# A trunk of Mamba-2, attention and FFN layers: weight loads on ScalarE's queue, scratch tensors in the reader's layout, decay work recorded later

## The chip, the cores and the metric

The kernel runs on one core of a Trainium2 chip. The metric is the device time of one execution in microseconds (us): 3116.06 us before, the median of three runs (3113.17 to 3118.34). The execution that was profiled took 3113.31 us; its span, from the first to the last instruction, is 3111.6 us. Everything is computed in float32. To keep the accuracy, each large matrix product is made of three matmuls on reduced-precision parts: a tensor `t` is split into a high part and the remainder, and the product is high x high + high x low + low x high.

Engines: PE is TensorE (matmul), ACT is ScalarE, DVE is VectorE, POOL is GpSimd, SP is SyncE. SP does no arithmetic; in the kernel before it issues almost all DMAs. Each engine takes its instructions in the order in which they stand on it, and one that waits holds up all behind it.

## The reference, cut to what matters

One sequence of 1024 tokens with 1024 channels passes four residual layers: Mamba-2 mixer, FFN, attention, FFN. The change lies mostly in the mixer:

```
def ssd_mixer(xn, in_w, ...):
    proj = xn @ in_w                       # z, xbc, dt
    xbc = silu(causal_dwconv(xbc, conv_w, conv_b))     # 4 taps along time
    dt = softplus(dt + dt_bias); a = -exp(a_log)
    a_cs = cumsum(dt * a) inside a chunk
    lmat = exp(a_cs[l] - a_cs[s]) for l >= s, else 0   # decay inside the chunk
    y_diag = (C B^T * lmat) @ (x * dt)
    states = B, decay to the chunk's end, x * dt ; h = scan over the chunks
    y_off = C @ h_in * exp(a_cs)
    y = (y_diag + y_off + x * d_skip) * silu(z)
    return (rmsnorm of y inside each of 4 groups * norm_g) @ out_w

x = x + ssd_mixer(rmsnorm(x), ...);   x = x + conv_ffn(rmsnorm(x), ...)
x = x + diff_attention(rmsnorm(x), ...);  x = x + conv_ffn(rmsnorm(x), ...)
```

There are 32 heads of 64 channels in 4 groups of 8 heads; the state has 128 columns; B and C are shared inside a group.

## The kernel before

**Tiles and passes.** Channels lie on the 128 partitions, time on the free axis, in two halves of 512 tokens. A weight block is 128 output channels by 1024 inputs: `split_weight` loads it (`ws`), ACT casts the high part (`wh`, L96), POOL subtracts to get the low part (`wl`, L98). `ws`, `wh` and `wl` have two buffers each. A pass is one 128x128 piece of the weight against 512 tokens: three matmuls (L276 to L278). A projection unit is eight passes into one PSUM tile, after which its end function (`xbc_end`, `z_end`, `out_end`) copies the result out and works on it.

**The mixer's stream.** `Stream` writes the projection passes out one after another, with hooks between them. First come the 40 blocks of the input projection, group by group: six of xbc and four of z. After an xbc block ACT and DVE run the convolution and SiLU (L415 to L427) and SP writes the block to the DRAM scratch `xbc_d` (L428); z blocks go to `z_d` (L439). Then come the 32 blocks of the output projection.

**The core in slots.** The recurrence is worked out in chunks of 128 tokens: 4 groups x 8 chunks are 32 slots, s = 0 to 31, spread between the passes of the stream: 20 passes to a slot for the first 24, 14 for the last eight. For a slot, `core_load` brings `xc` (six blocks of xbc, L539) and `seg` (the cumulated decays of 8 heads, broadcast to all partitions, L541), and records the decay chain: POOL subtracts (L542), ACT applies relu and exp (L543, L544). `core_load_out` brings `er` (L553) and `zc` (L555). `core_tokens` transposes B and x on PE (`pb`, `px`, L568 to L572), copies `btok` on ACT (L574), makes `cbm` and `xdt` on DVE (L576, L579), `xdec` on POOL (L581) and multiplies `seg` by `cbm` on DVE (L582). `core_out` has the products: `pd` (y_diag, L600, reads that `seg`), `po` (y_off, L604), `pst` (the new state, L608), then the sums on DVE and POOL (`y`, L616 to L620; `hn`, L613, L614). The gate multiplies by `zc`, writes `y_d` (L630) and sums squares into `ss` (L632 to L634); after each fourth chunk `group_stats` takes the column sums on PE (`tst`, L149). `out_load` reads `y_d` back as `yb` (L660), scales it and splits it into `xh` and `xl` (L663 to L665) for the output projection.

**What sets the order.** The code records the instructions in a program order; the tile framework's scheduler then sets each engine's own order from it and from the dependencies, so that an instruction can stand earlier on its engine than in the code. A load recorded two slots ahead waits on SP for its buffer (`xc` and `seg` have three) and for whatever stands before it on SP. The four PSUM buffers of the core (`cps`) go round among `pb`, `px`, `pd`, `po`, `pst`, `tst` and others in the order in which they are asked for.

**Attention** runs its projections and output projection through the same `Stream`, between the tiles of scores.

## Time and profile before

| | |
|---|---|
| median of three runs | 3116.06 us |
| the profiled execution, own time / span | 3113.31 us / 3111.6 us |
| mixer, up to the end of the output projection | about the first 940 us |
| busy over the span: PE, DVE, ACT, POOL | 94%, 59%, 34%, 35% |
| the chain that ended last, by engine | PE 67%, DVE 13%, DMA 7%, POOL 4%, issue 3%, ACT 3% |

The profile's page cuts the span in 40 slices. PE is busy in 100% of nearly every slice of the two FFN layers, in some 94% in attention, and least in the mixer. Busy time is only half of what to read there: TensorE's granted clock is the other. Its two levels are 2.4 and 1.2 GHz, shown as 1.00 and 0.50, and the mean over a stretch says how much of it ran at the lower one. A wait is told by the engine that idled, the instruction that ended the idling, and the one that released it. For DMAs the page gives the median time from issue to landing.

### The profile page before, as it was taken

Reading aid. Unit: us, or ns where it says so; the run is one execution under the profiler, and the core shown is the slowest. Engines: PE = TensorE matmul, PEld = TensorE weight load, DVE = VectorE, ACT = ScalarE, POOL = GpSimd, SP = SyncE. Lnnn points to the kernel's source line nnn. Section 1 sums busy time; section 2 is a strip of 40 time slices with the busy share of each in tenths; the row PEclk is TensorE's granted clock in tenths of the full one; section 3 lists DMA queues with packets and bytes.
Section 4 is the critical chain, followed back from the end, with each engine's and each line's share of the span. In section 5 each row is a group of like instructions: output and inputs, shape, how many; then the busy total and the mean of one; then the engine's idle time right before and its main releaser. Section 6 shows DMA issues by size and latency. Waiting matters only on the chain.

```text
span 3111.6 us, 35613 instructions
## 1 busy us (share of the span) xinstructions
PE 2927.5 (94%) x13636; PEld 2312.8 (74%) x13636; DVE 1826.6 (59%) x2880; ACT 1064.2 (34%) x1767; POOL 1076.3 (35%) x776
## 2 busy tenths in 40 slices
PE   7998888887899999999998999999999999999999
PEld 5777677665678888888886666666677888888887
DVE  6436464554666544435357788888867635344354
ACT  4433343433333221212123555555544312122121
POOL 3235454545544222222223633343435222222222
PEclk9999999998899999999999999999999999999999
DMA  3445455556432111111113221122442111111113
GB/s 102 132 122 150 131 144 155 126 158 160 139 107 68 48 48 48 48 48 49 53 39 117 74 57 55 55 61 55 119 144 69 54 48 49 54 48 48 48 45 105
DMA packets 196762, 262.77 MB, mean 84 GB/s; under 512 B 17777, under 2 KB 132977, under 8 KB 196593
## 3 DMA queue, kind: packets, MB, share of 16 engines
q1 hardware_dynamic: 187760, 244.77, 26.1%
q0 software_dynamic: 8832, 15.73, 2.1%
q8 instruction: 107, 1.75, 0.2%
q14 instruction: 63, 0.51, 0.1%
HBM read 206.39 MB, written 45.68 MB: 81 GB/s over the span
## 4 chain that ended last, share of the span: by engine, by line
PE 67%; DVE 13%; DMA 7%; POOL 4%; issue 3%; ACT 3%; SPq 0%; POOLq 0%; ACTq 0%; DVEq 0%
PE mm L112 10%; PE mm L113 10%; PE mm L111 10%; PE dp L112 5%; PE dp L113 5%; PE dp L111 5%; PE mm L276 5%; PE mm L277 5%; PE mm L278 5%; DMA seg<-acs_d 4%; PE s L1120 2%; PE s L1119 1%; POOL seg L542 1%; DVE nb L1122 1%; DVE nb L1123 1%
## 5 line engine op out<-in xcount | busy, mean ns | idle before, releaser
L98 POOL TENSOR_TENSOR wl<-ws,wh 128x1024 fp32r<-128x1024 f32 (+2 forms) x272 | 611.7, 2249 | 1154.8 <-ACT wh L96 1144.9
L276 PE MATMUL mm<-xh,wh 128*128 128x512 f32 x1280 | 539.8, 423 | 16.0 <-ACT xh L664 10.7
L112 PE MATMUL mm<-xl,wh 128*128 128x512 f32 x1408 | 549.1, 390 | 0.6 <-POOL xl L238 0.6
L113 PE MATMUL mm<-xh,wl 128*128 128x512 f32 x1408 | 548.9, 390 | 0.3 <-POOL wl L98 0.3
L111 PE MATMUL mm<-xh,wh 128*128 128x512 f32 x1408 | 548.8, 390 | 0.0
L278 PE MATMUL mm<-xh,wl 128*128 128x512 f32 x1280 | 512.8, 401 | 7.9 <-POOL wl L98 7.9
L277 PE MATMUL mm<-xl,wh 128*128 128x512 f32 x1280 | 513.8, 401 | 3.1 <-DVE xl L238 2.4
L96 ACT CAST wh<-ws 128x1024 fp32r<-128x1024 f32 (+2 forms) x272 | 266.9, 982 | 677.3 <-PE dp L112 296.5
L773 DVE TENSOR_SCALAR cv<-raw,fcw,fcb 128x1024 f32<-128x1024 f32 x88 | 214.9, 2442 | 405.3 <-ACT raw L768 405.3
L276 PEld LDWEIGHTS mm<-xh,wh 128*128 128x128 f32 x1280 | 247.6, 194 | 83.3 <-issue 18.9
L112 PEld LDWEIGHTS mm<-xl,wh 128*128 128x128 f32 x1408 | 265.0, 188 | 57.2 <-POOL xl L238 2.2
L113 PEld LDWEIGHTS mm<-xh,wl 128*128 128x128 f32 x1408 | 264.9, 188 | 55.8 <-POOL wl L98 0.8
L111 PEld LDWEIGHTS mm<-xh,wh 128*128 128x128 f32 x1408 | 265.0, 188 | 54.9
L278 PEld LDWEIGHTS mm<-xh,wl 128*128 128x128 f32 x1280 | 246.7, 193 | 63.0 <-POOL wl L98 10.5
L277 PEld LDWEIGHTS mm<-xl,wh 128*128 128x128 f32 x1280 | 247.3, 193 | 61.7 <-issue 9.1
L809 DVE TENSOR_TENSOR x<-x,dp 128x512 f32<-128x512 f32 x192 | 130.6, 685 | 245.7 <-PE dp L113 245.7
L112 PE MATMUL dp<-al,wh 128*128 128x512 f32 x704 | 274.0, 389 | 0.0
L111 PE MATMUL dp<-ah,wh 128*128 128x512 f32 x704 | 273.9, 389 | 0.0
L113 PE MATMUL dp<-ah,wl 128*128 128x512 f32 x704 | 273.9, 389 | 0.0
L775 DVE SCALAR_TENSOR_TENSOR cv<-raw,fcw,cv 128x1024 f32<-128x1024 f32 x176 | 230.1, 1307 | 12.8 <-DVE cv L773 1.4
L768 ACT COPY raw<-mm 128x512 f32<-128x512 f32 x176 | 101.5, 577 | 189.0 <-PE mm L113 189.0
L421 DVE SCALAR_TENSOR_TENSOR cv<-raw,cw,cv 128x1024 f32<-128x1024 f32 x72 | 111.4, 1548 | 91.3 <-ACT cv L419 61.7
(244 smaller groups left out, 4079.6 us busy)
## 6 DMA issues: line engine op xcount, KB each, us to landing
ws<-in_ffn_up_w_dram SPq DMA_DIRECT2D x88, 512.0 KB, 3.5
ws<-in_ssd_in_w_dram SPq DMA_DIRECT2D x40, 512.0 KB, 3.6
seg<-acs_d SPq DMA_DIRECT2D x32, 512.0 KB, 9.6
ws<-in_ssd_out_w_dram SPq DMA_DIRECT2D x32, 512.0 KB, 3.5
ws<-in_ffn_down_w_dram SPq DMA_DIRECT2D x32, 512.0 KB, 3.4
xbc_d<-cv SPq DMA_DIRECT2D x24, 512.0 KB, 4.1
xc<-xbc_d SPq DMA_DIRECT2D x32, 384.0 KB, 8.0
ws<-in_attn_in_w_dram SPq DMA_DIRECT2D x24, 512.0 KB, 3.5
```

The costliest lines, as they stand in the source:

```text
L96: act.copy(wh[:, :n], ws[:, :n])
L98: pool.tensor_tensor(wl[:, :n], ws[:, :n], wh[:, :n], op=ALU.subtract)
L111: pe.matmul(ps, wh[:, m, k, :], xh, start=k == 0, stop=False)
L112: pe.matmul(ps, wh[:, m, k, :], xl, start=False, stop=False)
L113: pe.matmul(ps, wl[:, m, k, :], xh, start=False, stop=k == n - 1)
L276: pe.matmul(ps, wh[:, 0, k, :], xh, start=k == 0, stop=False)
L277: pe.matmul(ps, wh[:, 0, k, :], xl, start=False, stop=False)
L278: pe.matmul(ps, wl[:, 0, k, :], xh, start=False, stop=k == nk - 1)
L421: dve.scalar_tensor_tensor(cv, raw[:, 1 + k:1 + k + T], cw[:, i, k:k + 1], cv, op0=ALU.mult, op1=ALU.add)
L773: dve.tensor_scalar(cv, raws[b][:, 4:], cw[:, n, 2:3], cb[:, n:n + 1], op0=ALU.mult, op1=ALU.add)
L775: dve.scalar_tensor_tensor(cv, raws[b][:, 2 + k:2 + k + T], cw[:, n, k:k + 1], cv, op0=ALU.mult, op1=ALU.add)
L809: dve.tensor_tensor(x, x, ps, op=ALU.add)
```

## The change

Five things change in the code.

1. `split_weight` is parted: `load_weight` issues the load on a queue that is handed over, and `Stream` keeps `raw`, the loads made so far. Weights of the mixer and of attention are now issued by ACT; `weight(i)` also records the load of block i + 1. The FFN's weights stay on SP.
2. The scratch tensors have the reader's layout. `xbc_d`, `z_d`, `y_d` are stored by group and chunk, so that what a slot reads of one partition lies in one piece; `acs_d` too, with the heads of `er` put side by side. So `xc`, `seg`, `er`, `zc` and the write of `y_d` move one piece for each partition, where they moved 6, 8, 4, 4 and 4 pieces of 512 bytes. The writes of `xbc_d` and `z_d` move eight pieces of 512 bytes for each partition, where they moved one of 4 KB, and the read `yb` four, where it moved one of 2 KB. `acs_d` is written by 16 DMAs in place of two.
3. The decay chain is recorded by `core_decay` at the start of the slot before its use, no longer behind its load.
4. The group's statistics: every chunk has its own `tst` matmul and an ACT copy into `rstd` (`chunk_stats`), one slot later; after the fourth the rsqrt follows on DVE. `out_load(1, h)` moves to the next slot as well.
5. The step at 4/5 of a slot is gone; what it held is in `late`.

```diff
@@ -88,10 +88,16 @@
     gffn = load_const("norm_ffn_g", [P, DEPTH, KB])
-    def split_weight(src, kb, mb):
+    def load_weight(src, kb, mb, queue=None):
         n = kb * mb * P
         ws = wpool.tile([P, 1024], F32, name="ws", tag="ws")
-        sp.dma_start(ws[:, :n], src)
+        (queue or sp).dma_start(ws[:, :n], src)
+        return ws
+
+    def split_weight(src, kb, mb, ws=None):
+        n = kb * mb * P
+        if ws is None:
+            ws = load_weight(src, kb, mb)
         wh = wpool.tile([P, 1024], F32R, name="wh", tag="wh")
         act.copy(wh[:, :n], ws[:, :n])
         wl = wpool.tile([P, 1024], F32R, name="wl", tag="wl")
@@ -246,8 +252,9 @@
-        def __init__(self, wsrc):
+        def __init__(self, wsrc, queue):
             self.wsrc, self.w, self.units, self.hooks = wsrc, {}, [], []
+            self.queue, self.raw = queue, {}
         def add(self, w, nk, xs, end, ahead=0, ps_new=ps_mm):
@@ -257,9 +264,16 @@
             self.hooks.append((n, k, len(self.hooks), f))
             self.hooks.sort(key=lambda t: t[:3])
+        def load(self, i):
+            if i < len(self.wsrc) and i not in self.raw:
+                self.raw[i] = load_weight(*self.wsrc[i], 1, self.queue)
+
         def weight(self, i):
+
             if i is not None and i < len(self.wsrc) and i not in self.w:
-                self.w[i] = split_weight(*self.wsrc[i], 1)
+                self.load(i)
+                self.load(i + 1)
+                self.w[i] = split_weight(*self.wsrc[i], 1, self.raw[i])
             return self.w.get(i)
         def run_hooks(self, n, k):
@@ -362,16 +376,19 @@
             order += [("x", g * 6 + j) for j in (4, 5, 0, 1, 2, 3)] + [("z", g * GB + j) for j in range(GB)]
         xw += [(a["ssd_in_w"][i + (XBC_BLOCKS if kind == "z" else 0)], KB) for kind, i in order]
         xw += [(a["ssd_out_w"][q, m], KB) for q in range(2) for _ in range(2) for m in range(KB)]
-        stream = Stream(xw)
+        stream = Stream(xw, act)
         begin(stream)
         st = ExitStack()
         sb = st.enter_context(tc.tile_pool(name="ssd", bufs=2, reuse_waits="tile"))
         s1 = st.enter_context(tc.tile_pool(name="ssd1", bufs=1, reuse_waits="tile"))
         cps = st.enter_context(tc.tile_pool(name="cps", bufs=4, space=PSUM, reuse_waits="tile"))
-        xbc_d = dram.tile([XBC_BLOCKS, P, T], F32, name="xbc_d")
-        z_d = dram.tile([Z_BLOCKS, P, T], F32, name="z_d")
-        y_d = dram.tile([Z_BLOCKS, P, T], F32, name="y_d")
-        acs_d = dram.tile([2, HEADS, T], F32, name="acs_d")
+        xbc_d = dram.tile([GROUPS, NCH, P, GB + 2, CH], F32, name="xbc_d")
+        z_d = dram.tile([GROUPS, NCH, P, GB, CH], F32, name="z_d")
+        y_d = dram.tile([GROUPS, NCH, P, GB, CH], F32, name="y_d")
+        acs_d = dram.tile([2, GROUPS, NCH, HG, CH], F32, name="acs_d")
+
+        def chunks(t):
+            return t.rearrange("p (c l) -> p c l", l=CH)
         def one(name, shape):
             return s1.tile(shape, F32, name=name, tag=name)
@@ -425,7 +442,7 @@
                     th = nrm.tile([P, HT], F32, name="th", tag="sq", bufs=2)
                     act.activation(th, u, AF.Tanh)
                     dve.scalar_tensor_tensor(u, th, 1.0, u, op0=ALU.add, op1=ALU.mult)
-                sp.dma_start(xbc_d[i], cv)
+                sp.dma_start(xbc_d[i // 6, :, :, i % 6, :].rearrange("c p l -> p c l"), chunks(cv))
             return end
         def z_end(i, h, state):
@@ -436,7 +453,7 @@
                 act.activation(zt, ps, AF.Tanh, scale=0.5)
                 dve.scalar_tensor_tensor(zt, zt, 1.0, ps, op0=ALU.add, op1=ALU.mult)
                 if h == 1:
-                    sp.dma_start(z_d[i], state["t"])
+                    sp.dma_start(z_d[i // GB, :, :, i % GB, :].rearrange("c p l -> p c l"), chunks(state["t"]))
             return end
@@ -520,7 +537,14 @@
                     for c in range(4):
                         pe.matmul(ps[:, c * CH:(c + 1) * CH], dA[:, h * 4 + c, :], lhs, start=True, stop=True)
                     act.activation(dtT[:, h * HT:(h + 1) * HT], ps, AF.Exp if r else AF.Copy)
-                sp.dma_start(acs_d[r], dtT)
+                for g in range(GROUPS):
+                    for q in range(2):
+                        if r:
+                            src, dst = dtT[g * HG + q:(g + 1) * HG:2], acs_d[1, g, :, q * GB:(q + 1) * GB]
+                        else:
+                            m = g * HG + q * GB
+                            src, dst = dtT[m:m + GB], acs_d[0, g, :, q * GB:(q + 1) * GB]
+                        sp.dma_start(dst.rearrange("c h l -> h c l"), chunks(src))
             tabs["t"] = dt, col, dtd, cdec
         hst = {}
@@ -533,26 +557,31 @@
         def core_load(s):
             g, c, hs, cs = place(s)
-            col = tabs["t"][1]
             st = {}
             xc = st["xc"] = sb.tile([P, 6, CH], F32, name="xc", tag="xc", bufs=3)
-            sp.dma_start(xc, xbc_d[g * 6:(g + 1) * 6, :, cs].rearrange("b p t -> p b t"))
+            sp.dma_start(xc, xbc_d[g, c])
             seg = st["seg"] = sb.tile([P, HG, CH], F32, name="seg", tag="seg", bufs=3)
-            sp.dma_start(seg, acs_d[0, hs, cs].unsqueeze(0).to_broadcast([P, HG, CH]))
+            sp.dma_start(seg.rearrange("p h l -> p (h l)"),
+                         acs_d[0, g, c].rearrange("h l -> (h l)").unsqueeze(0).to_broadcast([P, HG * CH]))
+            return st
+
+        def core_decay(s, st):
+            g, c, hs, cs = place(s)
+            col, seg = tabs["t"][1], st["seg"]
             pool.tensor_tensor(seg, col[:, c, hs].unsqueeze(2).to_broadcast([P, HG, CH]), seg, op=ALU.subtract)
             act.activation(seg, seg, AF.Relu)
             act.activation(seg, seg, AF.Exp, scale=-1.0)
-            return st
         def core_load_out(s, st):
             g, c, hs, cs = place(s)
             er = st["er"] = sb.tile([P, GB, CH], F32, name="er", tag="er")
             for q in range(2):
-                src = acs_d[1, hs, cs].rearrange("(j q) t -> q j t", q=2)[q]
-                sp.dma_start(er[q * 64:(q + 1) * 64], src.unsqueeze(0).to_broadcast([64, GB, CH]))
+                src = acs_d[1, g, c, q * GB:(q + 1) * GB].rearrange("j l -> (j l)")
+                sp.dma_start(er[q * 64:(q + 1) * 64].rearrange("p j l -> p (j l)"),
+                             src.unsqueeze(0).to_broadcast([64, GB * CH]))
             zc = st["zc"] = sb.tile([P, GB, CH], F32, name="zc", tag="zc")
-            sp.dma_start(zc, z_d[g * GB:(g + 1) * GB, :, cs].rearrange("b p t -> p b t"))
+            sp.dma_start(zc, z_d[g, c])
         def core_tokens(s, st):
             g, c, hs, cs = place(s)
...
@@ -621,33 +650,32 @@
             h, hc = divmod(c, 4)
             if hc == 0:
-                sums[g] = nrm.tile([P, HT], F32, name="ss", tag="acc")
-            ss = sums[g]
-            csl = slice(hc * CH, (hc + 1) * CH)
+                rstd[g, h] = one(f"rs{g}{h}", [P, 4])
             def gate():
                 dve.tensor_tensor(y, y, zc, op=ALU.mult)
-                sp.dma_start(y_d[g * GB:(g + 1) * GB, :, cs].rearrange("b p t -> p b t"), y)
+                sp.dma_start(y_d[g, c], y)
                 sq = sb.tile([P, GB, CH], F32, name="sq", tag="yo", bufs=1)
                 act.activation(sq, y, AF.Square)
                 pool.tensor_tensor(sq[:, 0:2], sq[:, 0:2], sq[:, 2:4], op=ALU.add)
-                pool.tensor_tensor(ss[:, csl], sq[:, 0, :], sq[:, 1, :], op=ALU.add)
+                ss = sb.tile([P, CH], F32, name="ss", tag="ss")
+                pool.tensor_tensor(ss, sq[:, 0, :], sq[:, 1, :], op=ALU.add)
+                late.append(lambda: chunk_stats(g, h, hc, ss))
+                if hc == 3 and g == GROUPS - 1:
+                    late.append(lambda: out_load(1, h))
             pend.append(gate)
-            if hc == 3:
-                pend.append(lambda: group_stats(g, h, ss))
-                if g == GROUPS - 1:
-                    pend.append(lambda: out_load(1, h))
         def cnew(shape, name):
             return cps.tile(shape, F32, name=name, tag="c")
-        rstd = {}
-
-        def group_stats(g, h, ss):
-            r = token_stats(cnew, ss, 0.25 / (GB * P))
-            keep = rstd[g, h] = one(f"rs{g % 2}{h}", [P, 4])
-            dve.tensor_copy(keep, r)
+        def chunk_stats(g, h, hc, ss):
+            ps = cps.tile([P, 1], F32, name="tst", tag="c")
+            pe.matmul(ps, ss, ones[:, 0:1], start=True, stop=True)
+            act.copy(rstd[g, h][:, hc:hc + 1], ps)
+            if hc == 3:
+                r = rsqrt_small("rs", rstd[g, h], 4, 0.25 / (GB * P))
+                dve.tensor_copy(rstd[g, h], r)
         yp = {}
@@ -657,7 +685,7 @@
             for k in range(KB):
                 b = q * KB + k
                 t = sb.tile([P, HT], F32, name="yb", tag="raw")
-                sp.dma_start(t, y_d[b, :, h * HT:(h + 1) * HT])
+                sp.dma_start(chunks(t), y_d[b // GB, h * 4:(h + 1) * 4, :, b % GB, :].rearrange("c p l -> p c l"))
                 if k % GB == 0:
                     rs = token_spread(cnew, rstd[b // GB, h])
                 dve.scalar_tensor_tensor(t, t, ng[:, b:b + 1], rs, op0=ALU.mult, op1=ALU.mult)
@@ -713,7 +741,9 @@
         starts = [base + 20 * s if s < 24 else base + 480 + 14 * (s - 24) for s in range(SLOTS + 1)]
         stream.advance_to(base - 40)
         sts = {0: core_load(0)}
-        stream.advance_to(base - 20)
+        stream.advance_to(base - 28)
+        core_decay(0, sts[0])
+        stream.advance_to(base - 16)
         core_tokens(0, sts[0])
         sts[1] = core_load(1)
         core_load_out(0, sts[0])
@@ -721,7 +751,11 @@
             t0, L = starts[s], starts[s + 1] - starts[s]
             stream.advance_to(t0)
             core_out(s, sts[s])
+            if s + 1 < SLOTS:
+                core_decay(s + 1, sts[s + 1])
             stream.advance_to(t0 + L // 5)
+            while late:
+                late.pop(0)()
             pend.pop(0)()
             if s == 4:
                 extra()
@@ -731,10 +765,9 @@
                 core_load_out(s + 1, sts[s + 1])
             if s + 2 < SLOTS:
                 sts[s + 2] = core_load(s + 2)
-            stream.advance_to(t0 + 4 * L // 5)
-            while pend:
-                pend.pop(0)()
         stream.advance_to(starts[SLOTS])
+        while late:
+            late.pop(0)()
         stream.finish()
         st.close()
         tail.append(norms[1])
@@ -895,7 +928,7 @@
         wsrc = [(a["attn_in_w"][hd, w], KB) for hd in range(ATTN_HEADS) for w in (1, 0, 2)]
         wsrc += [(a["attn_out_w"][q, m], half) for q in range(2) for _ in range(2) for m in range(KB)]
-        stream = Stream(wsrc)
+        stream = Stream(wsrc, act)
         later = stream.later
         kv_even = pb = cos = sin = blk = gq = None
```

The scheduler's order shows three places, all in the second group of the mixer.

SP, slots 10 and 11 (in the trace before, this piece is issued from 418 to 440 us). `ws` is a weight load, `seg`, `xc`, `er` and `zc` are the core's loads. Before:

```order
L428 DMA xbc_d<-cv 128x1024
L94 DMA ws<-in_ssd_in_w_dram 128x1024
L541 DMA seg<-acs_d 128x8x128
L539 DMA xc<-xbc_d 128x6x128
L553 DMA er<-acs_d 64x4x128 x2
L428 DMA xbc_d<-cv 128x1024
L630 DMA y_d<-y 128x4x128
L555 DMA zc<-z_d 128x4x128
```

Now:

```order
L445 DMA xbc_d<-cv 128x8x128
L564 DMA seg<-acs_d 128x1024
L562 DMA xc<-xbc_d 128x768
L581 DMA er<-acs_d 64x512 x2
L445 DMA xbc_d<-cv 128x8x128
L657 DMA y_d<-y 128x512
L584 DMA zc<-z_d 128x512
```

The weight load is gone from between the block's write and the decay's load, and the pieces (the last two numbers of a shape) have changed as said.

ACT, slot 9, which starts at 383.95 us in the trace before. `wh` is the weight's cast, `cv` and `th` the convolution's, `btok` and `y` the next slot's, L543 and L544 (now L572 and L573) the decay's relu and exp. Before:

```order
L96 CAST wh<-ws 128x1024
L415 COPY raw<-mm 128x512
L632 ACTIVATE sq<-y 128x512
L419 ACTIVATE cv<-raw,cb,cw 128x1024
L543 ACTIVATE seg<-seg 128x1024
L595 ACTIVATE y<-xc,ssd_d 128x128
L544 ACTIVATE seg<-seg 128x1024
L574 COPY btok<-pb 128x128
L595 ACTIVATE y<-xc,ssd_d 128x128 x3
L415 COPY raw<-mm 128x512
L426 ACTIVATE th<-cv 128x512 x2
```

Now:

```order
L102 CAST wh<-ws 128x1024
L432 COPY raw<-mm 128x512
L659 ACTIVATE sq<-y 128x512
L436 ACTIVATE cv<-raw,cb,cw 128x1024
L675 COPY rs<-tst 128x1
L94 DMA ws<-in_ssd_in_w_dram 128x1024
L603 COPY btok<-pb 128x128
L624 ACTIVATE y<-xc,ssd_d 128x128 x4
L572 ACTIVATE seg<-seg 128x1024
L432 COPY raw<-mm 128x512
L443 ACTIVATE th<-cv 128x512 x2
L573 ACTIVATE seg<-seg 128x1024
```

Where `btok` stood behind the decay's relu and exp, it now stands behind a weight load, which waits for the `wl` that reads the same buffer. The scheduler sets this load as soon as it counts the buffer free, two or three instructions behind the cast.

POOL, the same slot. `y` and `hn` are the slot's sums, `seg` is the decay's subtraction, `wl` the low part of the weight just cast. Before:

```order
L620 TENSOR_TENSOR y<-y,yo 128x512
L613 TENSOR_TENSOR hn<-hn,cdec 128x512
L542 TENSOR_TENSOR seg<-col,seg 128x1024
L98 TENSOR_TENSOR wl<-ws,wh 128x1024
L633 TENSOR_TENSOR sq<-sq 128x256
```

Now:

```order
L649 TENSOR_TENSOR y<-y,yo 128x512
L642 TENSOR_TENSOR hn<-hn,cdec 128x512
L571 TENSOR_TENSOR seg<-col,seg 128x1024
L104 TENSOR_TENSOR wl<-ws,wh 128x1024
L660 TENSOR_TENSOR sq<-sq 128x256
```

Nothing has moved here: although the code records the subtraction later, it stands on POOL where it stood.

## Rows read from the trace of the kernel before

**Rows 1.** Stretches: us; busy PE, PEld, DVE, ACT, POOL; clock; DMA share, GB/s.

```profile
190.00:360.00 170.00, 146.97 (x751) 117.97 (x750) 85.65 (x106) 63.64 (x110) 79.72 (x60) 0.94 0.49 140
360.00:530.00 170.00, 146.65 (x750) 117.82 (x750) 90.25 (x121) 65.72 (x114) 81.40 (x61) 0.93 0.51 142
530.00:690.00 160.00, 134.26 (x662) 106.09 (x663) 93.84 (x128) 63.59 (x108) 76.11 (x54) 0.91 0.53 141
690.00:860.00 170.00, 136.80 (x653) 103.80 (x650) 97.25 (x148) 54.39 (x92) 88.26 (x58) 0.86 0.54 147
1100.00:1270.00 170.00, 170.00 (x752) 140.76 (x751) 72.52 (x58) 36.46 (x45) 39.18 (x25) 1.00 0.14 47
```

**Rows 2.** Waits of PE, 170 to 900 us: us in total, times, longest.

```profile
PE pd L600 <- DVE seg L582: 57.3, 13, 8.1
PE tst L149 <- POOL ss L634: 17.8, 4, 5.8
PE mm L276 <- ACT xh L664: 10.7, 2, 7.8
PE mm L278 <- POOL wl L98: 5.6, 3, 3.1
```

**Rows 3.** The same view of SP, POOL and ACT, one row each.

```profile
SPq L94 <- POOL wl L98: 254.3, 46, 11.6
POOL seg L542 <- DMA seg<-acs_d: 94.0, 23, 7.8
ACT seg L543 <- POOL seg L542: 153.5, 26, 11.1
```

**Rows 4.** Timeline: start, us, instruction, [idle before]; last: all of L600, first/last start.

```profile
360.13 0.48 PE L600 MATMUL pd<-seg,xdt 128*64 128x128 f32 x2 [8.13 <-DVE seg L582]
...
397.39 1.90 POOL L542 TENSOR_TENSOR seg<-col,seg 128x1024 f32<-128x1024 f32 x1 [6.50 <-DMA er<-acs_d]
399.33 1.06 ACT L543 ACTIVATE seg<-seg 128x1024 f32<-128x1024 f32 x1 [6.08 <-POOL seg L542]
405.31 0.33 PE L600 MATMUL pd<-seg,xdt 128*64 128x128 f32 x2 [2.26 <-DVE seg L582]
422.75 0.33 PE L600 MATMUL pd<-seg,xdt 128*64 128x128 f32 x2
...
L600 PE MATMUL pd<-seg,xdt x512: 272/273/476, 190.1 to 859.1; 128*64 128x128 f32 x171
```

**Rows 5.** DMA issues: count, KB each, median us from issue to landing.

```profile
ws<-in_ssd_in_w_dram SPq DMA_DIRECT2D x40, 512.0 KB, 3.6
seg<-acs_d SPq DMA_DIRECT2D x32, 512.0 KB, 9.6
...
xbc_d<-cv SPq DMA_DIRECT2D x24, 512.0 KB, 4.1
...
y_d<-y SPq DMA_DIRECT2D x32, 256.0 KB, 6.3
yb<-y_d SPq DMA_DIRECT2D x32, 256.0 KB, 3.5
```

**Rows 6.** Timeline of POOL and SP around 430 us.

```profile
427.59 2.41 POOL L98 TENSOR_TENSOR wl<-ws,wh 128x1024 fp32r<-128x1024 f32 x1 [1.96 <-ACT wh L96]
...
430.02 0.35 SPq L94 DMA_DIRECT2D ws<-in_ssd_in_w_dram  x1
430.47 0.37 SPq L541 DMA_DIRECT2D seg<-acs_d  x1
```

**Rows 7.** Groups by line, 190 to 860 us: count, busy us, mean ns, idle before.

```profile
L98 POOL TENSOR_TENSOR wl<-ws,wh 128x1024 fp32r<-128x1024 f32 x44 | 107.4, 2442 | 67.9 <-ACT wh L96 67.6 <-DMA yb<-y_d 0.2
```

**Rows 8.** Timeline of ACT and POOL in attention's output projection.

```profile
2283.77 0.62 ACT L96 CAST wh<-ws 128x512 fp32r<-128x512 f32 x1 [3.88 <-PE mm L277]
2285.99 0.88 ACT L1134 ACTIVATE p<-s,nb,rq 128x640 f32<-128x640 f32 x1 [1.60 <-DVE nb L1123]
...
2284.47 1.41 POOL L98 TENSOR_TENSOR wl<-ws,wh 128x512 fp32r<-128x512 f32 x1 [3.25 <-ACT wh L96]
```

More of the change, by code (lines that the diff above doesn't have):

```diff
@@ L582, in core_tokens @@
             dve.tensor_tensor(seg, seg, cbm.unsqueeze(1).to_broadcast([P, HG, CH]), op=ALU.mult)
-        sums = {}
+        rstd, late = {}, []
         def core_out(s, st):
```

## The prediction

> **What bounds the kernel now.** I read the stretches first. A stretch of the FFN has PE busy for 170.00 of 170 us at clock 1.00; the mixer's core, 190 to 860 us, has PE idle for 23.0 + 23.4 + 25.7 + 33.2 = 105.3 us in four stretches, with mean clocks of 0.94, 0.93, 0.91 and 0.86 [rows 1]. A mean clock of c means that 2(1 - c) of the time ran at 1.2 GHz: 20 + 24 + 29 + 48 = 121 us. The mixer's core is the place where time can be had, and PE is what waits there.
>
> How much it can give: the products `pd` of the 32 slots begin at 190.1 us and the last is at 859.1 us [rows 4], so 31 slots take 668 us (the last group's own 1 us taken off). A slot that nothing disturbed took 422.75 - 405.31 = 17.4 us [rows 4]. It has 20 passes of three matmuls, and a matmul takes 170/752 = 0.226 us at full clock [rows 1], so a slot with 14 passes would take 17.4 - 6 x 0.68 = 13.4 us. 24 x 17.4 + 7 x 13.4 = 511 us: the core loses 157 us, 105 by waiting and some 52 by the lower clock, a few products of `out_load` included.
>
> Then the waits. PE waits 57.3 us in 13 of the 32 slots for the product on DVE that `pd` reads, 17.8 us at four group ends for `ss`, 10.7 us for the first tiles of the output projection, 5.6 us for `wl` [rows 2]. DVE is busy for 55% of the four stretches and POOL for 49% [rows 1], so none of them is full; they wait in a row. ACT waits 153.5 us for POOL's subtraction, POOL 94.0 us of its own for the load of `seg`, SP 254.3 us with a weight load in hand for the buffer that `wl` reads [rows 3]. One slot shows the row: POOL stood 6.50 us for a load, subtracted, ACT's relu had stood 6.08 us and started at 399.33, and only behind it came `btok`, which DVE needs; `pd` started at 405.31, 2.26 us late [rows 4]. At 430 us SP's part shows: `wl` ends at 430.00, the weight load goes at 430.02, and the decay's load behind it at 430.47 [rows 6].
>
> **The change, part by part.**
>
> *Loads of the core.* A `seg` load of 512 KB in 1024 pieces of 512 bytes lands in 9.6 us, a weight of the same size in 128 pieces of 4 KB in 3.6; 256 KB in 512 pieces take 6.3 (`y_d`), in 128 pieces 3.5 (`yb`) [rows 5]. From 512 to 1024 pieces it is 3.3 us: 6.4 ns a piece. Counted by the tiles, a slot now sends 1024 + 768 + 512 + 512 + 512 = 3328 pieces for `seg`, `xc`, `er`, `zc` and `y_d`, some 21 us of the queue at that rate, in slots of 668/31 = 21.5 us: SP's queue is about full. After: 5 x 128 = 640 pieces, plus 10 blocks of 1024 in eight slots, 1280: 1920 pieces, 12 us. The price is that a block's write goes from 4.1 towards 9.6 us and that in many slots the `seg` load stands just behind such a write on SP. The new `seg` load takes between 3.6 (a weight's size and pieces) and 9.6 us (now; behind a write); I take 4 to 5, nearer the weight, since the pieces are a weight's. POOL's 94.0 us in 23 waits, 4.1 each, then go.
>
> What PE gets of it: each of the 13 `pd` can come 4.1 us earlier. Eight of the 13 waits are longer than that (8.1 the longest; 2.26 is one of the five shorter ones) and add up to 48 of the 57.3; 48 - 8 x 4.1 = 15 us stays. In the slot at 405.31 the new order costs something: `btok` stands behind a weight load of ACT, and this behind `wl`. With the load in time POOL's subtraction ends at 397.39 + 1.90 - 6.50 = 392.8, `wl` 2.4 us later [rows 7], the issue takes 0.35 as on SP [rows 6], so `btok` can start at 395.6; it started behind relu and exp, about 401.5. That is 5.9 us earlier against a wait of 2.26: covered. Term: -57 + 15 = **-42**.
>
> *Weights on ACT.* SP's 254.3 us in front of weight loads go from before the core's loads; that is the other half of the term above and not counted again. Of the 5.6 us for `wl` I take half, **-3**. ACT pays an issue and a wait for each weight. The rows have no such wait: at least nothing, at most the whole `wl`, 2.4 us for each of 44 weights in the core, 107 us of ACT [rows 7]. In the order two or three instructions of ACT lie between the cast and the load, so I take about 1 us each, beside the 94 us or so of waiting that ACT is freed of. In attention's output projection the cast at 2283.77 is followed by `wl` to 2285.88, and the next exp started at 2285.99, having waited for DVE [rows 8]: hidden there. For the tiles where it is not, **+5**, with 0 and 20 as its ends.
>
> For the weights the Trainium skill has a rule that speaks against the change: "DMA: Bandwidth & Descriptors", section "Issuing engines are not separate DMA queues", says that issuing from several engines saves only the sequencer's issue time, since all run on the same 16 DMA engines. Those are busy for 0.49 to 0.54 of the time here [rows 1], so by the rule the move would be worth 44 issues of 0.35 us, which are hidden, and the sum would keep its other terms. The 254.3 us are a wait of the sequencer and not a transfer, so I side with the row.
>
> *Statistics a slot later.* `tst` waited for `ss`, 17.8 us in four waits; a slot later `ss` is some 10 us old, so this goes. The `tst` tiles now go round with the other PSUM buffers, so that `px` needs `po`'s buffer, free when DVE has made `yo`; that is late in some slots, at least 0, at most the 17.8 gained; I take 3. **-15**.
>
> *Reading `y_d` back.* A `yb` load goes from 128 to 512 pieces, 3.5 to 6.3 us [rows 5]. Of eight loads for a half two are on their way at once; three pairs, 2.8 us each, lie behind the first: 8.4 us, exposed at the first half of the output projection where PE already waits 10.7 [rows 2]; the other halves have a projection's time ahead. **+8**, with 0 and 20 as its ends.
>
> *Clock.* Of 105.3 us of waiting 42 + 15 + 3 - 8 = 52 go, half. With them goes half of the 52 us lost at 1.2 GHz: **-26**, between 0 and -52.
>
> *At nothing:* 14 more issues for `acs_d`, ahead of the first `pd` at 190.1 us [rows 4], in a stretch with projections for PE alone; 32 copies of 128x1 on ACT, each under the 0.35 us of an issue, in ACT's idle time.
>
> Sum: -42 - 3 + 5 - 15 + 8 - 26 = -73. The profiled execution of 3113.3 us becomes 3040; the median of the runs stands 2.8 us above it, so **3043 us**. Late next: the first tiles of the output projection, and DVE's product in slots with a convolution.
>
> **The rivals.**
>
> *A: all but the output projection's start goes.* If loads were the only cause, 105.3 - 10.7 = 95 us of waiting and nine tenths of the clock's 52 go: -142 + 13 = -129, 2987 us. For it: the undisturbed slots of 17.4 us follow directly on disturbed ones. Against: some waits of `pd` are twice POOL's mean wait.
>
> *B: the loads stay late.* The writes of 1024 pieces stand in front of `seg` on the same queue, so it lands as late as now, and the order on POOL is unchanged, so the later recording does nothing. Left are -3 - 15 + 8 + 5 and 5 of clock: -10, 3106 us. For it: the order, SP's rows above all; against: 12 us of queue instead of 21 in a slot, and no such write in the last eight slots. The Trainium skill would bring the same result by another way: "DMA: Bandwidth & Descriptors", section "Specifications", gives 512 bytes as the size from which a transfer runs at line rate, by which the new layout would gain nothing. The 9.6 against 3.6 us for the same 512 KB [rows 5] say otherwise.
>
> *C: slower, ACT held by its own weight loads.* The place is the order of ACT in slot 9: a load waits for `wl`, `wl` for the subtraction, this for `seg`, and `btok` stands behind. If `seg` stays late, the 153.5 us of ACT's waits [rows 3] stay and up to 107 us come on top. PE paid 57.3 for 153.5, 0.37 of it: +40 us of `pd` waits, +8 and +5 as above, -18 of the statistics and `wl`, and half as much again by the clock on the 30 that are left of the mixer's: +50, 3166 us. It decides from the point where ACT's waits for POOL, of both kinds, exceed the 153.5 us of now by some 15.
>
> **How the numbers follow.** The forecast, 3000 to 3085, has 0.62; A 0.13, B 0.14, C 0.11. About 6 us (0.2%) is what a measurement of this kernel can tell from no change. Faster: 0.62 + 0.13 + half of B, 0.08: 0.83. Same: 0.05 of B and 0.01 of C: 0.06. Slower: 0.10 of C and 0.01 of B: 0.11. The range of 2985 to 3112 takes in A's value, the ends of the terms for ACT and `yb`, and B's value; it leaves out C and the far side of A.
>
> **What would show it.** Right: `seg` lands in under 6 us and POOL's waits for it fall below 30 us; PE's waits for `pd` fall below 20 us, those at `tst` are gone; most slots take 17.4 to 18.5 us; the clock of the four stretches is above 0.95. Wrong: writes of `xbc_d` at over 10 us with `seg` behind them (B); ACT with over 150 us of waits for POOL, at the weight loads and the decays (C); attention more than 10 us longer than before; waits for `yb`'s tiles above 25 us. If PE's waits go and the time does not, the clock's share was wrong.

## The result and the profile after

The changed kernel takes 3044.25 us (median of 4 runs, 3042.7 to 3050.4), the kernel before 3114.61 (4 runs, 3113.15 to 3118.34): ratio 0.9776, 95% interval 0.9759 to 0.9793. The forecast was 3043. The number came out; of the terms that make it up, several did not, and they cancelled.

The time by stage, of the profiled executions, worked out from the starts of the first and last `pd` and of the first and last matmul of each FFN's up-projections (us):

| kernel | to the first pd | core | output projection | FFN | attention | FFN | span |
|---|---|---|---|---|---|---|---|
| before | 190.1 | 669.1 | 99.1 | 655.7 | 766.6 | 731.0 | 3111.6 |
| changed | 187.0 | 583.8 | 102.2 | 655.8 | 782.0 | 731.1 | 3042.0 |

(The attention column begins at the last up-projection of the first FFN, so some 70 us of that layer's end lie in it.) The core lost 85.3 us, attention gained 15.4. First the core, in four stretches and one of the FFN, to be read against [rows 1]; columns as there.

```profile
200.00:340.00 140.00, 132.54 (x707) 106.15 (x706) 85.59 (x102) 60.81 (x111) 77.62 (x56) 0.99 0.51 162
340.00:490.00 150.00, 139.51 (x725) 112.77 (x723) 91.55 (x120) 65.96 (x120) 81.80 (x60) 0.98 0.52 159
490.00:640.00 150.00, 136.74 (x705) 108.01 (x704) 107.98 (x137) 63.49 (x116) 81.11 (x56) 0.97 0.51 162
640.00:770.00 130.00, 117.16 (x591) 91.43 (x589) 101.24 (x137) 53.87 (x98) 85.23 (x58) 0.92 0.57 178
1000.00:1170.00 170.00, 170.00 (x751) 140.77 (x751) 68.53 (x59) 32.91 (x40) 36.68 (x23) 1.00 0.15 50
```

PE still idles 7.5, 10.5, 13.3 and 12.8 us in them, and the clock is back to 0.97 and more except in the last. The waits of PE, POOL, ACT and SP between 170 and 900 us (SP's to 860), against [rows 2, 3]:

```profile
PE pd L629 <- DVE seg L611: 14.8, 6, 3.9
PE pd L629 <- issue: 11.4, 3, 5.2
PE pd L629 <- ACT y L624: 3.3, 1, 3.3
PE mm L292 <- POOL wl L104: 2.2, 3, 1.4
PE mm L290 <- ACT xh L692: 0.4, 1, 0.4
POOL seg L571 <- DMA seg<-acs_d: 32.1, 11, 4.8
ACT seg L572 <- POOL seg L571: 80.2, 26, 7.5
ACT btok L603 <- POOL wl L104: 20.2, 4, 6.8
SPq L445 <- DVE cv L444: 121.8, 18, 15.4
```

The waits for `pd` went from 57.3 to 29.5 us (for 11.4 of them the profile names no releaser), that for `xh` from 10.7 to 0.4, and none at a group's `tst` is left. SP waits for data to write, no longer with a weight load in hand. One slot of the chain, to be read against the slot in [rows 4]: start, us, engine, line, and in brackets the idle time before.

```profile
397.05 0.32 SPq L564 DMA_DIRECT2D seg<-acs_d  x1
406.50 2.34 POOL L571 TENSOR_TENSOR seg<-col,seg 128x1024 f32<-128x1024 f32 x1
408.87 1.06 ACT L572 ACTIVATE seg<-seg 128x1024 f32<-128x1024 f32 x1 [4.04 <-POOL seg L571]
411.31 0.25 ACT L603 COPY btok<-pb 128x128 f32<-128x128 f32 x1
413.71 1.09 PE L629 MATMUL pd<-seg,xdt 128*64 128x128 f32 x16
```

POOL finds the load there. In the 11 slots where it did wait for it, the subtraction began 3.5 to 7.5 us after the load's issue (median 5.8); before, the load alone took 9.6 [rows 5]. (For the loads of the changed kernel the page has no landing times.) A slot of some 17.7 us from one `pd` to the next now recurs, but 12 of the first 24 slots are still longer than 18.5.

Attention: the same place in a head, the changed kernel first, then the one before.

```profile
1758.55 1.24 ACT L1014 CAST Q<-qg 64x512 fp32r<-64x512 f32 x2
1761.93 1.26 ACT L1014 CAST K<-qg 64x512 fp32r<-64x512 f32 x2 [2.15 <-POOL qg L1001]
1764.05 0.88 ACT L1167 ACTIVATE p<-s,nb,rq 128x640 f32<-128x640 f32 x1 [0.86 <-DVE rsh L183]
1766.52 0.47 PE L191 MATMUL rb<-dg,ones_r 128*128 128x512 f32 x1 [2.04 <-DVE nb L1156]
```

```profile
1842.68 1.24 ACT L981 CAST Q<-qg 64x512 fp32r<-64x512 f32 x2
1846.47 0.89 ACT L1134 ACTIVATE p<-s,nb,rq 128x640 f32<-128x640 f32 x1 [2.55 <-DVE rsh L177]
1847.35 1.24 ACT L981 CAST K<-qg 64x512 fp32r<-64x512 f32 x2
1848.37 0.47 PE L185 MATMUL rb<-dg,ones_r 128*128 128x512 f32 x1 [0.22 <-DVE dg L183]
```

Two instructions of ACT have changed places: the exp `p` now stands behind the cast of K, which waits for POOL; and PE waits 2.04 us at `rb`, where it waited 0.22. The rows show both, but not that one made the other: the cast ends at 1763.19, and `p` starts only 0.86 us later, when DVE is ready. No load stands between these rows.

### The profile page after: what moved, and what is told of

It reads as the page before. It is cut to its first block, busy times and chain, and to the rows that moved or that the text cites. A ratio compares the mean times of both kernels' runs of the same rounds, so it can differ in the third digit from the quotient of the medians.

```text
span 3042.0 us, 35719 instructions
## 1 busy us (share of the span) xinstructions
PE 2906.2 (96%) x13636; PEld 2298.4 (76%) x13636; DVE 1863.6 (61%) x2880; ACT 1068.0 (35%) x1797; POOL 1081.7 (36%) x776
## 4 chain that ended last, share of the span: by engine, by line
PE 74%; DVE 13%; POOL 4%; DMA 4%; ACT 3%; issue 3%; SPq 0%; ACTq 0%; POOLq 0%; DVEq 0%
PE mm L118 10%; PE mm L119 10%; PE mm L117 10%; PE mm L290 6%; PE mm L291 6%; PE mm L292 6%; PE dp L118 5%; PE dp L119 5%; PE dp L117 5%; PE s L1153 2%; DVE cv L438 1%; PE s L1152 1%; POOL wl L104 1%; DVE dg L189 1%; PE po L633 1%
## 5 line engine op out<-in xcount | busy, mean ns | idle before, releaser
L118 PEld LDWEIGHTS mm<-xl,wh 128*128 128x128 f32 x1408 | 264.9, 188 | 57.3 <-POOL xl L244 2.3
L438 DVE SCALAR_TENSOR_TENSOR cv<-raw,cw,cv 128x1024 f32<-128x1024 f32 x72 | 123.0, 1710 | 52.7 <-ACT cv L436 25.6
```

What stands on the lines that cost most here:

```text
L118: pe.matmul(ps, wh[:, m, k, :], xl, start=False, stop=False)
L438: dve.scalar_tensor_tensor(cv, raw[:, 1 + k:1 + k + T], cw[:, i, k:k + 1], cv, op0=ALU.mult, op1=ALU.add)
```

## The experiments

Each was timed in three rounds beside the kernel before, whose median on these chips was 3119.5 to 3122.1 us; so ratios to it are compared (changed kernel: 0.9776 [0.9759, 0.9793]). The question: which part of the change made the core faster, and what attention paid for. The stage times given below are each of one profile.

**The layout undone, all else as changed (m_layout).** All of the diff's part 2 taken back.

> The changed kernel with the DRAM scratch laid out as before (512-byte pieces for seg, xc, er, zc, y_d; 128 pieces for block writes and yb loads). Theory 1, the pieces fill SP's queue: seg lands in about 9 us again, POOL waits over 70 us for it, the slots take 620 to 655 us, total 3085 to 3120, about 3100. Theory 2, 512 bytes already run at line rate, the layout is worth nothing: 3044 within 6. Theory 3, the writes of 1024 pieces and the 512-piece yb loads cost as much as the loads gain: 3035 to 3050.

3130.43 us, 1.0028 [1.0014, 1.0042]: all the gain is gone, and time and core lie above theory 1's ranges. Core 663.2 us, attention 782.1. Waits as above, then DMAs (count, KB, median us to landing):

```profile
POOL seg L563 <- DMA seg<-acs_d: 131.3, 26, 10.5
ACT seg L564 <- POOL seg L563: 157.1, 26, 11.3
PE pd L620 <- DVE seg L602: 69.0, 17, 7.6
```

```profile
seg<-acs_d SPq DMA_DIRECT2D x32, 512.0 KB, 9.7
xbc_d<-cv SPq DMA_DIRECT2D x24, 512.0 KB, 3.2
xc<-xbc_d SPq DMA_DIRECT2D x32, 384.0 KB, 8.4
er<-acs_d SPq DMA_DIRECT2D x64, 128.0 KB, 7.5
yb<-y_d SPq DMA_DIRECT2D x32, 256.0 KB, 3.1
```

With `seg` at 9.7 us, the weights' move, the later decay and the new statistics together are worth 5.9 us of the core, and the rest of the kernel gives back more.

**The layout alone, on the kernel before (p_layout).**

> The kernel before with the new layout of the DRAM scratch alone (weights on SP, decay behind its load, statistics by group). Theory 1, the layout is nearly the whole gain and the parts add: 3044 less the 14 us that ACT's weights cost in attention, plus some 11 us for the mixer's weights on SP, plus 15 for the statistics: 3056 (3048 to 3068). Theory 2, the parts need each other (a weight load on SP in front of a decay recorded at its load): 3075 to 3095. Theory 3, the layout gains nothing by itself: 3114.

3035.11, 0.9735 [0.9715, 0.9755]: faster than the whole change, and below the 3048 to 3068 of theory 1, the lowest that was expected. Core 592.1, output projection 99.1, attention 766.9. POOL waits 24.4 us for `seg`, although SP waits 290.1 us with weight loads in hand as before:

```profile
SPq L94 <- POOL wl L104: 290.1, 58, 10.7
...
POOL seg L566 <- DMA seg<-acs_d: 24.4, 9, 4.8
PE pd L625 <- issue: 33.0, 11, 7.2
PE tst L155 <- POOL ss L659: 1.4, 3, 0.6
```

**Half of the layout: `acs_d` alone in the changed kernel (l_acs), alone on the kernel before (p_acs), and all but `acs_d` (l_xzy).** 

> The changed kernel with the new layout only for acs_d (seg and er); xbc_d, z_d and y_d as before, so that xc, zc and y_d move 512-byte pieces, 2048 + 160 pieces for a slot where the changed kernel has 1920 and the kernel before 3328. Theory 1, the count of pieces on SP's queue sets how late loads come, and seg no longer stands behind writes of 1024 pieces: 3036 to 3055. Theory 2, xc in 768 pieces (8.4 us) comes late for the transposes and the B C product: 3070 to 3110. Theory 3, the layouts of both halves are needed equally: about 3085.

> The kernel before with the new layout for acs_d alone: seg and er come in 128 pieces each (er in two loads of 64), 16 small writes in place of two, all else as before. Theory 1, the late seg is the whole cause: POOL's waits for seg fall from 94 to about 25 us, core 580 to 590 us, total 3018 to 3036. Theory 2, SP's queue was full, and the 2208 pieces a slot still hold back xc and the block writes behind weight loads: 3050 to 3080.

> The changed kernel with the layout of acs_d undone alone (seg in 1024 pieces, er in 512; xc, zc, y_d in 128 as changed, block writes in 1024): 3200 pieces for a slot where m_layout has 3328 + 160. Theory 1, the late seg is the whole cause: like m_layout, and later by the writes of 1024 pieces in front of seg, POOL waits 130 us or more for it, 3125 to 3150. Theory 2, both halves of the layout carry part of the gain: 3080 to 3105.

l_acs 3045.09, 0.9761 [0.9741, 0.9781]; p_acs 3036.80, 0.9720 [0.9699, 0.9740]; l_xzy 3137.75, 1.0049 [1.0033, 1.0065]. So `acs_d` carries the gain with and without the other parts, and the layout of `xbc_d`, `z_d` and `y_d` adds nothing that these runs can tell, although it takes 288 pieces from a slot's queue. l_acs and l_xzy came out in theory 1's range; p_acs lies 0.8 us above it, its core of 599.6 above the 580 to 590 expected, in a profile of the slowest of its four runs (3045.24). l_xzy also shows landings with the pieces exchanged, to be read against those of m_layout:

```profile
seg<-acs_d SPq DMA_DIRECT2D x32, 512.0 KB, 9.9
xbc_d<-cv SPq DMA_DIRECT2D x24, 512.0 KB, 3.5
xc<-xbc_d SPq DMA_DIRECT2D x32, 384.0 KB, 8.3
yb<-y_d SPq DMA_DIRECT2D x32, 256.0 KB, 3.2
```

A block's write lands in 3.5 us in 1024 pieces and in 3.2 in 128; `yb` in 3.2 in 512 and 3.1 in 128; `xc`, which goes out behind `seg`, in 8.3 in 128 and 8.4 in 768. So for these three the count of pieces hardly shows.

**One size (best_seg_old against best).** The fastest version, below, with only this changed (and with it `seg`'s write, one DMA in place of eight):

```
-  sp.dma_start(seg, acs_d[0, g, c] ...)      # 128 pieces of 4 KB
+  sp.dma_start(seg, seg_d[hs, cs] ...)       # 1024 pieces of 512 bytes
```

> The fastest kernel so far (label best, 3023 us) with one size changed: seg is read from a tensor of its own in the layout before, in 1024 pieces of 512 bytes in place of 128 of 4 KB; er and all else stay. Theory 1, it is seg's own landing that POOL, ACT, DVE and PE wait for one after the other: POOL waits over 85 us for it again (20 in best), the core takes 640 us or more (574), total 3085 to 3115. Theory 2, it is the room on SP's queue, to which er's 512 pieces belong as well: a part comes back, core 590 to 620 us, total 3040 to 3070.

3117.46, 0.9991 [0.9976, 1.0007]; best has 0.9682 [0.9664, 0.9701]. One load's pieces are worth 94 us, more than the whole change: the core takes 661.3 us against 574.0, and the first `pd` comes 6.4 later. That is above theory 1's range.

```profile
POOL seg L573 <- DMA seg<-seg_d: 124.9, 24, 10.4
ACT seg L574 <- POOL seg L573: 169.4, 26, 12.2
PE pd L631 <- DVE seg L613: 56.5, 16, 6.9
PE tst L155 <- POOL ss L665: 16.6, 4, 6.3
```

```profile
seg<-seg_d SPq DMA_DIRECT2D x32, 512.0 KB, 9.9
```

(The trace has a landing for six of these 32 loads, 9.1 to 10.9 us.) The whole chain of [rows 2, 3] is back, the wait at `tst` with it. In best the same waits are:

```profile
POOL seg L571 <- DMA seg<-acs_d: 20.4, 7, 4.9
PE pd L629 <- issue: 20.9, 8, 5.5
PE tst L155 <- POOL ss L663: 0.5, 1, 0.5
```

**The mixer's weights back on SP (m_mix_sp):** `Stream(xw, act)` to `Stream(xw, None)`, without the load of block i + 1.

> The changed kernel with the mixer's weights issued by SP as before (no weight ahead there); attention as changed. Theory 1, the forecast's: SP's wait for wl with a weight load in hand stands in front of the core's loads; SP waits 150 us or more there again, POOL waits over 60 us for seg, the 31 slots take 610 to 640 us instead of 583, total 3060 to 3100, about 3075. Theory 2, issuing from another engine saves only issue time: 3044 within 6. Theory 3, ACT was held by its own weight loads in the core: faster, 3025 to 3038.

3053.86, 0.9789 [0.9761, 0.9817]: not told apart from the changed kernel by its ratio, and between the ranges of theories 1 and 2. In the one profile the core is 13.5 us longer and the stretch ahead of it 3.5 shorter; but SP's wait is all there, and POOL does not wait longer for `seg`, so theory 1's reason falls:

```profile
SPq L94 <- POOL wl L104: 278.3, 57, 10.8
...
POOL seg L572 <- DMA seg<-acs_d: 26.9, 11, 4.9
```

**The decay behind its load again (m_decay).**

> The changed kernel with the decay chain (subtract, relu, exp) recorded right behind its load again. Theory 1, the loads are in time by the layout and the weights' move: POOL and ACT meet seg about where it lands, total 3044 to 3060, about 3050. Theory 2, it is the half slot that hides the load, and what stands behind relu and exp on ACT (btok, hence DVE and pd) is held without it: POOL waits over 90 us for seg, ACT over 130 us for POOL, total 3075 to 3100.

3048.83, 0.9766 [0.9734, 0.9797]; core 584.1, POOL's wait for `seg` 26.0 us. Theory 1: the later recording is worth nothing that shows.

**The statistics by group again (m_stats).**

> The changed kernel with the group's statistics as before (four chunks summed into one tile, column sums at once at the end of a group's half). Theory 1, the forecast's: the waits of tst, 17.8 us in four waits before, come back, less some 3 us for the buffer: 3055 to 3065 with the clock. Theory 2, tst waited because the slot's end was late, and with the loads in time ss is there earlier too: 3044 to 3050.

3039.47, 0.9749 [0.9726, 0.9771]: no loss without the new statistics; if anything a gain (core 579.7, output projection 99.7), but the intervals overlap. PE waits 0.8 us at `tst`: theory 2's reason, with a time below its range.

**Attention's weights on SP (m_attn_sp):** `Stream(wsrc, act)` to `Stream(wsrc, None)`.

> The changed kernel with the attention weights issued by SP again, one weight ahead; the mixer as changed. Attention takes 695 us in the kernel before and 709 us in the changed one (from the first to the last mm of the two attention projections). Theory 1, ACT's weight loads (each behind a wait for wl) delay the softmax: attention falls back to 692 to 698 us, the total to 3030 us (3026 to 3034). Theory 2, the loss in attention comes from something else (the order in which it is entered, the clock): 3044 us, no change. Theory 3, one weight ahead on SP stands in front of the rk loads there: attention over 712 us, 3048 us or more.

3032.20, 0.9717 [0.9691, 0.9744]: attention 770.0, 12 us less. The loss is where theory 1 put it: in the six profiles with attention's weights on SP attention takes 766.6 to 772.8 us, in the seven with them on ACT 779.9 to 787.4. Whether for theory 1's reason, the next run asks.

**ACT waits, but keeps its order (a_dum_wait).** Attention's weights alone, with this line in front of each load:

```
+  act.copy(ws[:, 0:1], ident[:, 0:1])     # ACT waits for the buffer, as its own load would
   sp.dma_start(ws[:, :n], src)
```

> The changed kernel with the attention weights issued by SP, but each load preceded by a copy of one column into its buffer on ACT, so that ACT waits for the buffer as it does with its own load, while its other instructions keep the order of the kernel before; with ACT's own loads the scheduler puts exps of the softmax behind casts and copies that they stood ahead of. Theory 1, the changed order of ACT costs the 14 us in attention: attention 695 us, total 3030 (3026 to 3035). Theory 2, the waits and the extra instructions cost it: attention 705 to 710 us, total 3040 to 3046.

3037.62, 0.9741 [0.9724, 0.9757], attention 777.5: between the two theories. The cast of K stands behind `p` in six places, as in the kernel before (in one in the changed kernel). ACT does wait, 43.3 us, yet PE's waits are those of the kernel with the loads on SP, not those of the changed one. First a_dum_wait, then the changed kernel:

```profile
ACT ws L95 <- POOL wl L107: 43.3, 38, 2.4
ACT K L1017 <- POOL qg L1004: 6.0, 4, 3.4
PE vt L1030 <- DVE at L1201: 3.6, 6, 1.2
```

```profile
ACT K L1014 <- POOL qg L1001: 23.8, 9, 5.0
PE vt L1027 <- DVE at L1198: 7.2, 7, 1.1
PE rb L191 <- DVE nb L1156: 6.8, 5, 2.0
```

So something costs beside the waits: 0.9741 [0.9724, 0.9757] lies below the changed kernel's 0.9776. That is the order, or the issues' own time on ACT, which this run does not part from it (54 issues take 18.1 us of ACT in the changed kernel's attention, the 53 copies here 10.0). Whether the waits cost too stays open: m_attn_sp's interval reaches up to 0.9744.

**A faster version (best):** `acs_d` alone in the new layout, attention's weights on SP, the statistics as before; the mixer's weights on ACT and the later decay kept.

> The parts that the runs so far show as gains, put together: the new layout for acs_d alone (xbc_d, z_d, y_d as before), the mixer's weights on ACT, the decay recorded later; the attention weights on SP and the statistics by group as before. Theory 1, the parts add by stages of the traces (start 187, core 573 - 4, output projection 99.5, FFN 656 and 731, attention 768 us): span 3011, total 3012 (3006 to 3020). Theory 2, the gains of l_acs and m_stats in the core are one and the same (long slots made shorter): 3020 to 3030.

3023.26, 0.9682 [0.9664, 0.9701]; start 188.3, core 574.0, output projection 99.7, attention 771.1. It beats both kernels; theory 2, since the parts of l_acs and m_stats in the core did not add.

One comparison bears on the mixer's weights. p_acs and best differ only in these weights' queue, in one weight load ahead (attention's too, where the profiles differ by 1.7 us) and in the later decay, and were timed in the same rounds: 3032.2 to 3045.2 us in the four runs of p_acs, 3019.6 to 3028.2 in those of best, 13.5 us between the medians. m_decay gives the later decay nothing in the changed kernel, so most of it is likely the weights'. The profiles agree: with `seg` in 128 pieces the core takes 592.1 to 599.6 us in the three kernels with the mixer's weights on SP, 573.1 to 584.7 in the seven with them on ACT.

## Why the forecast was right, and which of its steps were not

The mechanism was right: a late `seg` held POOL, ACT, DVE and PE in a row, and its layout in 1024 pieces was what made it late. best_seg_old shows that by itself. That the sum came within 2 us was luck in part, since errors of its terms cancelled. Term by term:

- *Loads, -42.* The waits for `pd` fell by 28 us, not 42; but the same cause was also behind the statistics' wait and most of the clock's share, which I had priced as causes of their own. The core's four terms (-42, -3, -15, -26) add to -86; it lost 85.3 us, of which 77.0 come with the layout alone (p_layout) and 69.5 with that of `acs_d` alone (p_acs). What failed is the queue as the reason ("SP's queue is about full"): with 2208 pieces for a slot (l_acs) the kernel is as fast as with 1920, so the queue's fill in these bounds sets nothing, and the 6.4 ns a piece are not a price of pieces: a block's write in 1024 of them lands in 3.5 us (l_xzy), where I had it go towards 9.6. Whether 896 pieces less in other loads would have helped a `seg` of 1024 was not tried; 288 less (l_xzy) did not.
- *Weights on ACT, "the other half of the term above".* Not that half. SP's 254.3 us look like the largest wait of the mixer, and p_layout keeps 290.1 of them while POOL's wait for `seg` falls from 94.0 to 24.4: a load that lands fast can go out behind the weight. But the move is not worth nothing either, as p_acs against best shows; what in the core it shortens stays open (POOL's wait for `seg` is 28.3 us in p_acs and 20.4 in best). The Trainium skill, "DMA: Bandwidth & Descriptors", section "Issuing engines are not separate DMA queues", says that another engine saves issue time only; I sided against it. m_mix_sp can't decide that (0.9789 against 0.9776), and whether the 13.5 us between p_acs and best are more than issue time was not traced.
- *ACT's price, +5, up to 20.* Attention took 15.4 us more in the profile, and m_attn_sp gives 12 back. The step that failed is "hidden there": it was read from one tile of the output projection in the old trace, which can't show that the scheduler would put the softmax's exps behind casts that wait for POOL. The order of the changed kernel on ACT would have shown it. That this order is the cost is likely by a_dum_wait, but not parted from the issues' own time.
- *Statistics, -15.* Wrong in kind. `ss` was late because the slot was: 0.8 us at `tst` in m_stats, 16.6 in best_seg_old, where `seg` is late again. The 17.8 us belonged to the first term.
- *`yb`, +8.* Nothing: the output projection takes 99.1 us in p_layout, with reads in 512 pieces, and 99.1 in the kernel before, with 128; such a read lands in 3.2 us in l_xzy, not in the 6.3 I took. The 3.1 us more in the changed kernel come with the new statistics: 101.9 to 103.6 us in the eight kernels that have them, 99.1 to 99.7 in the six that don't.
- *Clock, -26.* Too small. The time at 1.2 GHz in the core, added up from the clock's record, went from 119.5 to 41.0 us, which gives back up to 39 (less where PE idled in it); with `seg` late again it is 109.2 (best_seg_old), against 37.5 in best.
- *"Late next".* The first tiles of the output projection are not (`xh` 0.4 us); `pd` in slots with a convolution is (25 of its 29.5 us of waits).

So the core's forecast stood with its parts in the wrong places. Outside it the output projection lost 3.1 us in place of 8, attention lost 15.4 in place of 5, and the start gained 3.1 that no term had. Of the marks set, `seg` (by the 5.8 us above), `tst` and the waits for `yb` came out; missed were POOL's waits (32.1 against 30), `pd` (29.5 against 20), the length of the slots, the last stretch's clock (0.92), and attention's 10 us.

The rivals: B falls, since the loads came early with writes of 1024 pieces in front; of it only "the later recording does nothing" is true (m_decay). By the Trainium skill, the same page, section "Specifications", 512-byte pieces run at line rate, and the layout would gain nothing. For the block's writes and `yb` the landings in l_xzy and m_layout agree with it, and their layout gained nothing; for `seg`, 0.9991 against 0.9682 says otherwise. C's place is wrong: even with `seg` late (m_layout) the core is 5.9 us shorter than before, not 40 longer. Its sign came true there, 1.0028, by attention. A's 2987 was not reached by any version: best still has PE idle for 36.8 us of the core, added up from its rows.

## What to carry to other kernels

Waits in a row can have one cause: price the earliest late arrival, and do not add prices for the waits that follow from it, however large each is in the list. Here a load that is broadcast and that many engines wait for was worth storing so that it is read in long pieces; for the other transfers it changed nothing that shows. And an issue moved to another engine can change that engine's order, so read the new order wherever the engine is waited for, not only where the issue lands.

## What the runs showed of the hardware that was not expected

How long a transfer took to land did not follow from its pieces. 512 KB in 1024 pieces of 512 bytes took 9.6 to 9.9 us as `seg`, which is broadcast to all partitions, in all four kernels that had it, but 3.5 us as the write of a block (l_xzy), where the same block in 128 pieces of 4 KB took 3.2 (m_layout). 256 KB of `yb` took 3.2 us in 512 pieces and 3.1 in 128. So the forecast's 6.4 ns a piece, taken between two kinds of transfer, does not describe that. What makes `seg` pay for short pieces, the broadcast, the direction or its neighbours on the queue, was not tried.
